# Hybrid gMLP/GLA encoder layer on one core: the first block's z weights split in three, three and two pieces, the low-rank part one slot later, the first output tile's product one slot sooner

## The chip, the cores and the metric

The kernel runs on one core of a Trainium2 chip. The metric is the device time of one execution in microseconds (us). The engines are PE (TensorE: matmuls), ACT (ScalarE), DVE (VectorE), POOL (GpSimd) and SP (SyncE, which here issues every transfer). Each works through its own instructions in order, so an instruction that waits also holds back everything behind it on its engine.

## The reference

One layer is applied to a prompt of 512 positions and to a sample of 2048, both 1024 wide:

```
h = rmsnorm(x) * norm_pre
p = h @ w_in                      # columns: u, v, z (512 each), q, k (256 each), v_b, z_b (512 each), lr_f, lr_b (16 each)
A = gelu(u) * (w_sp @ layernorm(gelu(v)) + b_sp) * silu(z)      # per chunk of 128 positions, 4 heads
g = log_sigmoid(lr @ w_gk + b_gk) / 16                          # forward and backward
B = rmsnorm(gla(q, k, v_b, g_f) + gla_reversed(q, k, v_b, g_b)) * silu(z_b)
y = x + rmsnorm(concat(A, B) @ w_out) * norm_post
```

## The kernel before

The 2560 positions are five blocks (b = 0 to 4) of 512. Every float32 operand of the large products is split into a high and a low float16 part, and three products (high by high, high by low, low by high) replace one. So a projection of 128 rows or 128 columns by 512 over the depth of 1024 is 24 matmuls of 128x512 (8 depth pieces by 3), which accumulate in one PSUM buffer.

`slot()` is the unit of the schedule, and it is written by hand. In each slot the generators already under way take one step each (older projections first, then pieces of weight preparation named by the table `pre`, then the list `early`, then `aux`, then the pieces named by `bg`), after that the slot's own projection is issued on PE, and last `flush()` issues the smaller matmuls that the steps have left in `late`. A step emits instructions in program order to every engine, so the slot at which a step runs fixes its place in each engine's queue.

The first block has 20 slots: z_b in slots 0 to 3, v_b 4 to 7, u 8 to 11, q/k 12 to 15 (`pqk`, column groups 0, 2, 1, 3), z 16 to 19 (`pz`). Later blocks have 24 slots: v (`pv`) 0 to 3, z_b (`pzb`) 4 to 7, v_b 8 to 11, q/k 12 to 15, then u and z in turn.

A projection writes to a buffer of the pool `pj`, which has two; the projection of slot s + 2 can start only when the buffer of slot s has been read out. The read-outs are: for q/k four `scalar_tensor_tensor` on DVE (L494, into the tiles QE and KE); for z a tanh on ACT (L447) and then a multiply on DVE (L448), after which POOL multiplies by gelu(u) (L449); one slot later DVE (L460, L462) joins this with the spatial product `sv`, and ACT squares it (L463) into the same buffer `th`, of which there is one.

In the first block the weights are also split. `g_wprep("z")` first finds a scale; then each of its eight steps splits one depth piece k of 128 rows: ACT writes the high part (L218), DVE the low part (L219). `pz` of slot 16 uses the pieces in the order k = 0 to 7, three matmuls each.

While block b runs, `g_xprep(b + 1, i)` prepares the next block's input for its four row tiles i. Its steps are: the load of x (L133); a square with a row sum on ACT (L119) that writes its unneeded result into the tile `xs`; a scaled copy on ACT (L138) into `xs`; the low part on DVE (L140), and two transposing transfers out of `xs` into `hT` (L129). The pool of x and xs has two buffers, so the square of tile i writes where the transposing transfers of tile i - 1 read. For block 1 the steps begin in slots 9, 12, 14 and 16 of block 0.

`g_lr` makes the low-rank part: 64 small matmuls (L511, `plr`), a copy on ACT (L517), some work with 16 transposes on DVE (L530), then copies into the tile `lr` (L534, L535), in three successive slots; `g_gates` multiplies `lr` by the gate weights (L558, `pg`) at the end of its first slot.

After block 4 the output projection follows: `g_out(t)` prepares output tile t (load, state, the product `oi` on PE, L797 and squares, then the products L809 to L815, which the table calls step five, then transposing transfers L819), and `g_main(t, n)` issues the 24 matmuls `py` (L844) for each half.

Of the kernel before, what the change touches and what calls it, by code (L numbers as in the profile page):

```python
# [35 lines left out]
def tile_hybrid_gmlp_gla(ctx: ExitStack, tc: tile.TileContext, x_prompt, x_sample, norm_pre, w_in,  # L36
# [359 lines left out]
    vb = [None] * NB  # L396
# [30 lines left out]
    def g_v(b, i):  # L427
        ps = proj_tok(b, i, W["v"], f"pv{b}_{i}")
        yield
        v = v_stats(b, i, v_gelu(b, i, ps, ("gu", "th")[i % 2]))  # L430
        yield
        v_split(b, i, *v)
# [36 lines left out]
    def g_zb(b, i):  # L469
        ps = proj_tok(b, i, W["zb"], f"pzb{b}_{i}")  # L470
        yield
        th = tp.tile([P, BT], F32, name=f"tb{b}_{i}", tag=TB_TAGS[b][i % len(TB_TAGS[b])])
        nc.scalar.activation(th, ps, AF.Tanh, scale=EVH["zb"])  # L473
        nc.vector.scalar_tensor_tensor(th, th, 1.0, ps, op0=ALU.add, op1=ALU.mult)  # L474
        yield
        nc.sync.dma_start(out=scr[b][:, i, 2, :], in_=th)

    def g_vb(b, i):
        ps = proj_tok(b, i, W["vb"], f"pvb{b}_{i}")
        yield  # L480
        if i == 0:
            vb[b] = bp.tile([P, 4, 512], F32, name=f"vb{b}", tag="big8")
        nc.scalar.activation(vb[b][:, i, :], ps, AF.Copy, scale=EV["vb"])

    def g_qk(b, c):
        ps = proj_ch(b, W["qk"], c * P, f"pqk{b}_{c}")
        yield
        dst = QE[b] if c < 2 else KE[b]
        s = EVH["qk"] if c < 2 else EV["qk"]
        for hh in range(2):  # L490
            h = 2 * (c % 2) + hh
            for d in range(2):
                o = dst[64 * d:64 * d + 64, h, :]
                nc.vector.scalar_tensor_tensor(o, ps[64 * hh:64 * hh + 64, :], s[64 * d:64 * d + 64], o,  # L494
                                               op0=ALU.mult, op1=ALU.mult)
        yield
        if c == 1:
            for i in range(4):
                nc.sync.dma_start(out=scr[b][:, i, 1, :].rearrange("p (h t) -> p h t", t=P),
                                  in_=QE[b][:, :, i * P:(i + 1) * P])  # L500
# [200 lines left out]
    def g_wout_bound(n, half, j):  # L701
        r = wout_piece(n, half, j, "wob")
        yield
        nc.scalar.activation(r, r, AF.Abs, scale=C["gnorm"] if half else 1.0,
                             accum_out=sumO[:, half, 2 * n + j:2 * n + j + 1])
# [117 lines left out]
    def out_step(t):  # L823
        if t < NT:
            if t not in outs:
                outs[t] = g_out(t)
            next(outs[t], None)
        return
        yield
# [222 lines left out]
    b = 0  # L1052
# [6 lines left out]
             16: [g_gla(b, 0), g_xprep(1, 3)], 18: [g_gla(b, 1)]}  # L1059
    first = {0: [g_v0_stats()], 5: [g_gates(b)]}  # L1060
    tiny = {0: ["vb"], 1: ["vb"], 2: ["u"], 3: ["u"], 5: ["qk", "sp"], 6: ["qk", "sp"], 10: ["z"], 12: ["z"]}
    pre = {2: [("vb", 4)], 3: [("vb", 5)], 13: [("z", 2)], 14: [("z", 2)], 15: [("z", 2)], 16: [("z", 2)]}
    plan = {1: [("u", 1)], 3: [("qk", 1)], 4: [("u", 4), ("qk", 1), ("sp", 1)], 5: [("u", 5)], 7: [("qk", 4)],
            8: [("qk", 5), ("sp", 1)], 9: [("sp", 2), ("z", 1)]}
    for s, u in enumerate(units):
# [7 lines left out]
    for b in range(1, NB):  # L1073
        units = ([g_v(b, i) for i in range(4)] + [g_zb(b, i) for i in range(4)] + [g_vb(b, i) for i in range(4)]
                 + [g_qk(b, c) for c in (0, 2, 1, 3)] + [f(b, h) for h in range(H) for f in (g_u, g_z)])
        extra = {}
        gates = {0: [g_lr(b)], 4: [g_gates(b)]}
        if b == 1:
            gates = {3: [g_lr(b)], 6: [g_gates(b)]}

        def at(s, *gens):
            extra.setdefault(s, []).extend(gens)

        chunks = [(b, i, 16 + 2 * i) for i in range(4)]
        if b == 1:
            chunks += [(0, 2, 0), (0, 3, 2)]
        for bb, i, s in chunks:
            at(s, g_gla(bb, i))
        if b in (1, 2):
            for s, piece in zip((19, 20, 21, 22), wo_pieces[4 * (b - 1):]):  # L1090
                at(s, g_wout_bound(*piece))
        if b == 3:
            at(12, g_wout_scale())
            for s, piece in zip((19, 20, 21, 22), wo_pieces):
                at(s, g_wout(*piece))
        if b < NB - 1:
            for i, s in enumerate((1, 6, 11, 15)):
                at(s, g_xprep(b + 1, i))
        else:
            for s, piece in zip((12, 13, 14, 15), wo_pieces[4:]):  # L1100
                at(s, g_wout(*piece))
            at(6, g_out_scale(0, NB - 1))
            at(14, g_npost())
            for s, t in ((17, 0), (18, 0), (19, 0), (19, 1), (20, 0), (20, 1), (21, 1), (22, 1), (22, 0), (23, 0)):
                at(s, out_step(t))
        for s, u in enumerate(units):
            if b == NB - 1 and s == 17:
                R3["OT"] = wp.tile([P, 4, KC, 2, P], F16, name="OT", tag="W")
            slot(u, new=extra.get(s, ()), first=gates.get(s, ()))
# [4 lines left out]
    for s in range(2 * NT):  # L1114
        t, n = s // 2, s % 2
# [43 lines left out]
```

## Time and profile before

| | |
|---|---|
| time, median of 3 runs | 980.91 us (980.67 to 981.34) |
| the profiled execution | 981.4 us, of which the span of the trace is 979.7 us |
| PE busy | 960.5 us, 98% of the span |
| DVE, ACT, POOL busy | 576.4, 418.9, 213.8 us |
| idle time of the matmul row, by what ended it | 5.9 us `pz` behind ACT's w_z; 1.0 and less for every other |

The busy time of PE is the sum of its matmul records, and a record runs on while the next begins. The rows of the sections below give a start, a length, the engine, the line, the operation and the tiles; in brackets stands the idle time of the engine before it and what ended that.

### The profile page before, as it was taken

Reading aid. Unit: us, or ns where it says so; the run is one execution under the profiler, and the core shown is the slowest. Engines: PE = TensorE matmul, PEld = TensorE weight load, DVE = VectorE, ACT = ScalarE, POOL = GpSimd, SP = SyncE. Lnnn points to the kernel's source line nnn. Section 1 sums busy time; section 2 is a strip of 40 time slices with the busy share of each in tenths; the row PEclk is TensorE's granted clock in tenths of the full one; section 3 lists DMA queues with packets and bytes.
Section 4 is the critical chain, followed back from the end, with each engine's and each line's share of the span. In section 5 each row is a group of like instructions: output and inputs, shape, how many; then the busy total and the mean of one; then the engine's idle time right before and its main releaser. Section 6 shows DMA issues by size and latency. Waiting matters only on the chain. (4 is left out here: it accounts for less than half of the span.)

```text
span 979.7 us, 14266 instructions
## 1 busy us (share of the span) xinstructions
PE 960.5 (98%) x5485; PEld 506.5 (52%) x5485; DVE 576.4 (59%) x1105; ACT 418.9 (43%) x795; POOL 213.8 (22%) x258
## 2 busy tenths in 40 slices
PE   8999979999999999999999999999999999999997
PEld 7744435654455544465544456444555545554444
DVE  6765764456655636655645757554666656566553
ACT  6779633534423363124363233353144344344341
POOL 1030202322011313021312112311123232322231
PEclk9999989999999999999999999999999999999999
DMA  9622134222332122333121332021415798767952
GB/s 321 227 71 80 44 86 108 96 89 55 86 108 91 61 76 65 86 108 108 43 86 43 87 118 87 33 76 44 172 65 199 216 260 258 223 220 224 248 163 97
DMA packets 113668, 120.71 MB, mean 123 GB/s; under 512 B 62784, under 2 KB 86208, under 8 KB 111040
## 3 DMA queue, kind: packets, MB, share of 16 engines
q1 hardware_dynamic: 113600, 119.80, 39.6%
q8 instruction: 43, 0.70, 0.3%
q14 instruction: 25, 0.20, 0.1%
HBM read 69.44 MB, written 36.70 MB: 108 GB/s over the span
## 5 line engine op out<-in xcount | busy, mean ns | idle before, releaser
L380 PEld LDWEIGHTS <-hT 128*128 128x128 f16 x1344 | 130.4, 98 | 157.5 <-issue 3.8
L844 PE MATMUL py<-wo,OT 128*128 128x512 f16 (+1 forms) x960 | 207.9, 376 | 0.0
L844 PEld LDWEIGHTS <-OT 128*128 128x128 f16 x984 | 96.3, 98 | 106.9
L390 PE MATMUL pz<-hT,w_z 128*128 128x512 f16 x480 | 108.5, 382 | 5.9 <-ACT w_z L218 5.9
L380 PE MATMUL pzb<-w_zb,hT 128*128 128x512 f16 x480 | 106.4, 379 | 1.0 <-DVE tb L474 1.0
L390 PE MATMUL pu<-hT,w_u 128*128 128x512 f16 x480 | 106.6, 379 | 0.0
L390 PE MATMUL pqk<-hT,w_qk 128*128 128x512 f16 x480 | 105.1, 379 | 0.5 <-DVE KE L494 0.5
L380 PE MATMUL pvb<-w_vb,hT 128*128 128x512 f16 x480 | 104.8, 379 | 0.0
L637 DVE STREAM_TRANSPOSE kt<-KE 32x128 f32<-32x128 f32 x224 | 67.8, 303 | 34.4 <-PE kv L671 31.4
L380 PE MATMUL pv<-w_v,hT 128*128 128x512 f16 x384 | 84.5, 379 | 0.4 <-ACT vf L406 0.4
L449 POOL TENSOR_TENSOR th<-th,gu 128x512 f32<-128x512 f32 x20 | 32.7, 1635 | 211.3 <-DVE th L448 211.3
L390 PEld LDWEIGHTS <-w_z 128*128 128x128 f16 x480 | 45.8, 98 | 60.8 <-ACT w_z L218 6.4
L390 PEld LDWEIGHTS <-w_qk 128*128 128x128 f16 x480 | 46.7, 98 | 56.7 <-DVE KE L494 1.0
L390 PEld LDWEIGHTS <-w_u 128*128 128x128 f16 x480 | 47.0, 98 | 55.9
L863 DVE TENSOR_TENSOR y<-py,npost 128x512 f32<-128x512 f32 (+1 forms) x40 | 27.4, 685 | 70.6 <-PE py L844 60.2
L463 ACT ACTIVATE th<-t 128x512 f32<-128x512 f32 x20 | 12.6, 630 | 129.9 <-DVE t L462 129.7
L860 ACT ACTIVATE junk<-py 128x512 f16<-128x512 f32 (+1 forms) x40 | 23.7, 591 | 85.7 <-DVE y L863 84.5
L474 DVE SCALAR_TENSOR_TENSOR tb<-tb,pzb 128x512 f32<-128x512 f32 x20 | 13.7, 687 | 56.5 <-ACT tb L473 56.4
L494 DVE SCALAR_TENSOR_TENSOR QE<-pqk,ev_qk,QE 64x512 f32<-64x512 f32 x40 | 30.0, 749 | 27.3 <-PE pqk L390 24.3
L590 POOL TENSOR_TENSOR KE<-QE 64x1024 f32<-64x1024 f32 x10 | 32.1, 3210 | 63.4 <-DVE QE L584 40.4
L119 ACT ACTIVATE xs<-x 128x1024 f16<-128x1024 f32 x16 | 16.8, 1051 | 62.7 <-DMA x<-in_x_sample_dram 28.4
L654 DVE COPY_PREDICATED pr<-jlec,X 128x512 f32<-128x512 int32 x20 | 14.6, 730 | 40.7 <-ACT pr L653 40.5
(310 smaller groups left out, 1359.6 us busy)
## 6 DMA issues: line engine op xcount, KB each, us to landing
L<-scr SPq DMA_DIRECT2D x20, 1280.0 KB, 6.7
out_dram<-y SPq DMA_DIRECT2D x19, 512.0 KB, 7.4
x<-in_x_sample_dram SPq DMA_DIRECT2D x16, 512.0 KB, 4.1
xres<-in_x_sample_dram SPq DMA_DIRECT2D x16, 512.0 KB, 8.2
scr<-tb SPq DMA_DIRECT2D x20, 256.0 KB, 2.0
scr<-QE SPq DMA_DIRECT2D x20, 256.0 KB, 3.1
scr<-t SPq DMA_DIRECT2D x20, 256.0 KB, 2.4
scr<-S SPq DMA_DIRECT2D x20, 256.0 KB, 2.0
```

The lines of the kernel that those rows point to most:

```text
L119: nc.scalar.activation(junk, xt, AF.Square, accum_out=ms)
L380: nc.tensor.matmul(ps, lhsT=hT[b][:, k, a, i * P:(i + 1) * P], rhs=w[:, k, c, :], start=(n == 0), stop=(n == 3 * KC - 1))
L390: nc.tensor.matmul(ps, lhsT=w[:, k, c, col:col + P], rhs=hT[b][:, k, a, :], start=(n == 0), stop=(n == 3 * KC - 1))
L449: nc.gpsimd.tensor_tensor(t, t, gus[b, h], op=ALU.mult)
L474: nc.vector.scalar_tensor_tensor(th, th, 1.0, ps, op0=ALU.add, op1=ALU.mult)
L494: nc.vector.scalar_tensor_tensor(o, ps[64 * hh:64 * hh + 64, :], s[64 * d:64 * d + 64], o, op0=ALU.mult, op1=ALU.mult)
L590: nc.gpsimd.tensor_tensor(Mv[64:128, h:h + 2], Av[64:128, h:h + 2, :, ::-1], mid[64:128, h:h + 2].to_broadcast([64, 2, 4, P]), op=ALU.subt ...
L637: nc.vector.transpose(out=kt[32 * c:32 * c + 32, :, d], in_=KE[b][d, :, i * P + 32 * c:i * P + 32 * c + 32])
L654: nc.vector.copy_predicated(pr, C["jmask"], X)
L844: nc.tensor.matmul(bank[:, cs], lhsT=OT[:, k, a, :], rhs=wo[n][:, k, c, cs], start=(m == 0), stop=(m == 3 * KC - 1))
L860: nc.scalar.activation(junk[:, cs], pss[j][:, cs], AF.Square, accum_out=ms[:, n + j:n + j + 1])
L863: nc.vector.tensor_tensor(y[:, n * 512:(n + 1) * 512][:, cs], pss[j][:, cs], npost[n][:, cs], op=ALU.mult)
```

## The change

Three edits of the slot tables.

```diff
-    pre = {2: [("vb", 4)], 3: [("vb", 5)], 13: [("z", 2)], 14: [("z", 2)], 15: [("z", 2)], 16: [("z", 2)]}
+    pre = {2: [("vb", 4)], 3: [("vb", 5)], 13: [("z", 3)], 14: [("z", 3)], 15: [("z", 2)]}
...
-        gates = {0: [g_lr(b)], 4: [g_gates(b)]}
+        gates = {1: [g_lr(b)], 4: [g_gates(b)]}
         if b == 1:
             gates = {3: [g_lr(b)], 6: [g_gates(b)]}
...
-            for s, t in ((17, 0), (18, 0), (19, 0), (19, 1), (20, 0), (20, 1), (21, 1), (22, 1), (22, 0), (23, 0)):
+            for s, t in ((17, 0), (18, 0), (19, 0), (19, 1), (20, 0), (20, 1), (21, 0), (21, 1), (22, 0), (22, 1)):
                 at(s, out_step(t))
```

The first edit moves z's pieces. On ACT, slots 13 to 17 of block 0, before (xs_1, xs_2 are row tiles 1 and 2 of block 1, w_z the pieces' high parts, th_0 the tanh of the first `pz`):

```order
L218 ACTIVATE w_z<-raw_z,nps_z 128x512 x2
L119 ACTIVATE xs_1_1313,xms_1_1314<-x_1_1266 128x1024
L218 ACTIVATE w_z<-raw_z,nps_z 128x512 x2
L138 ACTIVATE xs_1_1313<-x_1_1266,xms_1_1314 128x1024
L218 ACTIVATE w_z<-raw_z,nps_z 128x512 x2
L119 ACTIVATE xs_2_1390,xms_2_1391<-x_2_1352 128x1024
L218 ACTIVATE w_z<-raw_z,nps_z 128x512 x2
L138 ACTIVATE xs_2_1390<-x_2_1352,xms_2_1391 128x1024
L447 ACTIVATE th_0_1476<-pz_0_1439,ev_z 128x512
```

And with the change:

```order
L218 ACTIVATE w_z<-raw_z,nps_z 128x512 x3
L119 ACTIVATE xs_1_1315,xms_1_1316<-x_1_1266 128x1024
L218 ACTIVATE w_z<-raw_z,nps_z 128x512 x3
L138 ACTIVATE xs_1_1315<-x_1_1266,xms_1_1316 128x1024
L218 ACTIVATE w_z<-raw_z,nps_z 128x512 x2
L119 ACTIVATE xs_2_1394,xms_2_1395<-x_2_1356 128x1024
L138 ACTIVATE xs_2_1394<-x_2_1356,xms_2_1395 128x1024
L447 ACTIVATE th_0_1476<-pz_0_1439,ev_z 128x512
```

The last two pieces have moved from behind the square of row tile 2 to ahead of it. On DVE in the same slots, before (KE, QE: the read-outs of `pqk`; w_z the low parts):

```order
L219 SCALAR_TENSOR_TENSOR w_z<-raw_z,nps_z,w_z 128x512 x2
L608 TENSOR_TENSOR wst<-ab 64x12
L611 TENSOR_TENSOR wst<-ab 64x12
L494 SCALAR_TENSOR_TENSOR KE_974<-pqk_2_1318,ev_qk,KE_974 64x512 x4
L219 SCALAR_TENSOR_TENSOR w_z<-raw_z,nps_z,w_z 128x512 x2
L494 SCALAR_TENSOR_TENSOR QE_973<-pqk_1_1354,ev_qk,QE_973 64x512 x4
L219 SCALAR_TENSOR_TENSOR w_z<-raw_z,nps_z,w_z 128x512 x2
L140 SCALAR_TENSOR_TENSOR xs_1_1313<-x_1_1266,xms_1_1314,xs_1_1313 128x1024
L494 SCALAR_TENSOR_TENSOR KE_974<-pqk_3_1395,ev_qk,KE_974 64x512 x4
L219 SCALAR_TENSOR_TENSOR w_z<-raw_z,nps_z,w_z 128x512 x2
L448 SCALAR_TENSOR_TENSOR th_0_1476<-th_0_1476,pz_0_1439 128x512
```

And with the change:

```order
L219 SCALAR_TENSOR_TENSOR w_z<-raw_z,nps_z,w_z 128x512 x3
L608 TENSOR_TENSOR wst<-ab 64x12
L611 TENSOR_TENSOR wst<-ab 64x12
L494 SCALAR_TENSOR_TENSOR KE_974<-pqk_2_1320,ev_qk,KE_974 64x512 x4
L219 SCALAR_TENSOR_TENSOR w_z<-raw_z,nps_z,w_z 128x512 x3
L494 SCALAR_TENSOR_TENSOR QE_973<-pqk_1_1358,ev_qk,QE_973 64x512 x4
L219 SCALAR_TENSOR_TENSOR w_z<-raw_z,nps_z,w_z 128x512 x2
L140 SCALAR_TENSOR_TENSOR xs_1_1315<-x_1_1266,xms_1_1316,xs_1_1315 128x1024
L494 SCALAR_TENSOR_TENSOR KE_974<-pqk_3_1399,ev_qk,KE_974 64x512 x4
L448 SCALAR_TENSOR_TENSOR th_0_1476<-th_0_1476,pz_0_1439 128x512
```

One low part more stands ahead of the first KE, two ahead of QE, and two ahead of the low part of xs_1 and the second KE. The second edit, on ACT in slots 1 to 3 of block 4, before (vf: the read-outs of `pv`, two halves each; lrt and lr: the low-rank part; va: the float16 copies of vf):

```order
L406 ACTIVATE vf_0_5391<-pv_0_5278,ev_v_445 128x256
L517 ACTIVATE lrt_5401<-plr_5271,ev_lr 128x256
L682 ACTIVATE S_5274<-kv_5276 64x512
L684 ACTIVATE ob_5430<-o_5277 128x512
L424 ACTIVATE va_5458<-vf_0_5391 128x512
L406 ACTIVATE vf_1_5462<-pv_1_5432,ev_v_252 128x256
L406 ACTIVATE vf_1_5462<-pv_1_5432,ev_v_445 128x256
L534 ACTIVATE lr_5410<-lrtr_5411 64x512
L424 ACTIVATE va_5458<-vf_1_5462 128x512
```

And with the change:

```order
L406 ACTIVATE vf_0_5326<-pv_0_5277,ev_v_445 128x256
L682 ACTIVATE S_5273<-kv_5275 64x512
L684 ACTIVATE ob_5339<-o_5276 128x512
L424 ACTIVATE va_5431<-vf_0_5326 128x512
L406 ACTIVATE vf_1_5435<-pv_1_5341,ev_v_252 128x256
L406 ACTIVATE vf_1_5435<-pv_1_5341,ev_v_445 128x256
L517 ACTIVATE lrt_5445<-plr_5336,ev_lr 128x256
L424 ACTIVATE va_5431<-vf_1_5435 128x512
```

The copy out of `plr` now stands behind the second read-out of v instead of the first; its matmuls and DVE's 16 transposes move likewise, in blocks 2, 3 and 4 alone.

## Rows read from the trace of the kernel before

**Rows 1.** The page: the span, and the busy time of the engines with their share of it and their instructions.

```profile
span 979.7 us, 14266 instructions
PE 960.5 (98%) x5485; PEld 506.5 (52%) x5485; DVE 576.4 (59%) x1105; ACT 418.9 (43%) x795; POOL 213.8 (22%) x258
```

**Rows 2.** The waits of PE: who waited for whom, us in total, how often, longest.

```profile
PE pz L390 <- ACT w_z L218: 5.9, 1, 5.9
...
PE pqk L390 <- DVE KE L494: 0.5, 1, 0.5
PE pv L380 <- ACT vf L406: 0.4, 1, 0.4
```

**Rows 3.** The timeline of PE's matmuls, block 0 slots 15 to 19 and the first slots of block 1: start, length, instruction, count.

```profile
127.29 5.35 PE L390 MATMUL pqk<-hT,w_qk 128*128 128x512 f16 x24 [0.47 <-DVE KE L494]
132.48 4.05 PE L390 MATMUL pz<-hT,w_z 128*128 128x512 f16 x18
142.46 2.74 PE L390 MATMUL pz<-hT,w_z 128*128 128x512 f16 x6 [5.94 <-ACT w_z L218]
...
147.66 5.34 PE L390 MATMUL pz<-hT,w_z 128*128 128x512 f16 x24
...
153.51 5.34 PE L390 MATMUL pz<-hT,w_z 128*128 128x512 f16 x24
...
161.29 0.37 PE L642 MATMUL X<-QE,KE 64*128 64x128 f32 x1
...
162.88 5.34 PE L390 MATMUL pz<-hT,w_z 128*128 128x512 f16 x24
...
168.73 5.34 PE L380 MATMUL pv<-w_v,hT 128*128 128x512 f16 x24
...
178.09 10.52 PE L380 MATMUL pv<-w_v,hT 128*128 128x512 f16 x48
```

**Rows 4.** Stretches of one us: PE, PEld, DVE, ACT, POOL busy with counts, then the clock granted to PE (1.00 is 2.4 GHz), the transfers' share and their GB/s.

```profile
48.00:49.00 1.00, 0.43 (x4) 0.43 (x5) 0.97 (x3) 0.00 (x0) 0.52 (x3) 1.00 0.00 0
139.00:140.00 1.00, 0.00 (x0) 0.00 (x0) 0.00 (x0) 0.00 (x0) 0.00 (x0) 1.00 1.29 267
140.00:141.00 1.00, 0.00 (x0) 0.00 (x0) 0.00 (x0) 0.35 (x1) 0.00 (x0) 0.70 1.15 346
147.00:148.00 1.00, 1.00 (x9) 0.70 (x7) 0.95 (x2) 0.74 (x2) 1.00 (x1) 0.88 0.00 0
```

**Rows 5.** The timeline of ACT from block 0 slot 13 to block 1 slot 0, with one instruction of POOL (the root of the row sum, between the square and the scaled copy).

```profile
121.75 1.33 ACT L218 ACTIVATE w_z<-raw_z,nps_z 128x512 f16<-128x512 f32 x2 [1.70 <-DVE nps_z L209]
...
140.65 1.06 ACT L119 ACTIVATE xs<-x 128x1024 f16<-128x1024 f32 x1 [13.03 <-DMA hT<-xs]
...
142.16 0.55 POOL L124 TENSOR_TENSOR xms<-xms,neghalf 128x1 f32<-128x1 f32 x1
...
142.93 1.13 ACT L138 ACTIVATE xs<-x,xms 128x1024 f16<-128x1024 f32 x1
145.24 0.69 ACT L447 ACTIVATE th<-pz,ev_z 128x512 f32<-128x512 f32 x1 [1.18 <-PE pz L390]
...
154.06 1.06 ACT L119 ACTIVATE xs<-x 128x1024 f16<-128x1024 f32 x1 [5.60 <-DMA hT<-xs]
155.02 0.19 ACT L119 ACTIVATION_READ_ACCUMULATOR xs<-x 128x1 f32 x1
155.35 0.63 ACT L463 ACTIVATE th<-t 128x512 f32<-128x512 f32 x1
...
156.10 0.69 ACT L447 ACTIVATE th<-pz,ev_z 128x512 f32<-128x512 f32 x1
...
171.50 0.69 ACT L447 ACTIVATE th<-pz,ev_z 128x512 f32<-128x512 f32 x1
```

**Rows 6.** The timeline of DVE in the same stretch.

```profile
122.51 1.42 DVE L219 SCALAR_TENSOR_TENSOR w_z<-raw_z,nps_z,w_z 128x512 f16<-128x512 f32 x2 [0.73 <-ACT w_z L218]
...
127.26 1.42 DVE L219 SCALAR_TENSOR_TENSOR w_z<-raw_z,nps_z,w_z 128x512 f16<-128x512 f32 x2
128.69 3.04 DVE L494 SCALAR_TENSOR_TENSOR QE<-pqk,ev_qk,QE 64x512 f32<-64x512 f32 x4
131.76 1.41 DVE L219 SCALAR_TENSOR_TENSOR w_z<-raw_z,nps_z,w_z 128x512 f16<-128x512 f32 x2
133.10 1.28 DVE L140 SCALAR_TENSOR_TENSOR xs<-x,xms,xs 128x1024 f16<-128x1024 f32 x1
...
146.57 1.28 DVE L140 SCALAR_TENSOR_TENSOR xs<-x,xms,xs 128x1024 f16<-128x1024 f32 x1
...
156.82 0.69 DVE L448 SCALAR_TENSOR_TENSOR th<-th,pz 128x512 f32<-128x512 f32 x1 [1.51 <-ACT th L447]
```

**Rows 7.** The timelines of DVE, ACT and PE, block 4 slots 1 to 4.

```profile
613.92 5.05 DVE L530 STREAM_TRANSPOSE lrtr<-lrk 32x128 f32<-32x128 f32 x16 [0.27 <-POOL lrk L523]
...
621.40 0.83 ACT L406 ACTIVATE vf<-pv,ev_v 128x256 f32<-128x256 f32 x2
...
632.45 0.81 PE L558 MATMUL pg<-lr,wg 128*128 128x512 f32 x2
```

**Rows 8.** The timeline of SP, the first output tile's transposing transfers; and the chain that ended last, the first matmuls of the output projection.

```profile
737.53 2.75 SPq L819 DMA_TRANSPOSE OT<-L  x2
...
747.68 5.18 PE py L844 x24
```

## Prediction

> **What bounds the kernel now.** I read the busy times first: PE is busy for 960.5 of 979.7 us [rows 1], so a change pays only where it removes time in which PE stands or runs slowly. The waits of PE came next: apart from the opening they hold one of any size, 5.9 us of `pz` behind ACT's w_z; those behind DVE's KE (0.5) and ACT's vf (0.4) are small [rows 2]. PE's timeline shows the place: the first `pz` starts at 132.48, stops after 18 of its 24 matmuls, which is six of eight depth pieces, and goes on at 142.46 after 5.94 us idle [rows 3]. ACT's timeline shows what is late: ACT stood for 13.03 us before the square of row tile 2 of block 1, which started at 140.65 and was released by the transposing transfers out of xs_1; the last two w_z pieces stand right behind it in program order. So the pieces were not dear, they were queued behind an instruction that waits for a transfer.
>
> The stop costs more than its length. The granted clock fell from 1.00 (2.4 GHz) towards 0.50 (1.2 GHz) at about 140.4 and was back late in 147 to 148 [rows 4]. From the start of the first `pz` to that of the second is 147.66 - 132.48 = 15.18 us [rows 3]. At full clock it is 5.19 (127.29 to 132.48, one projection start to start) plus the X, Y and transpose matmuls, 161.29 to 162.88 = 1.59 [rows 3], so 6.78. The loss is 8.40 us: 5.94 standing, 2.46 slow.
>
> **First edit: z in 3, 3, 2.** The number of instructions is the same; their places move. On ACT a piece takes 1.33 / 2 = 0.67 [rows 5]. ACT begins them at 121.75 and has no wait ahead of it until the square of tile 2, so all eight high parts, one square and one scaled copy end near 129. The 5.94 and the slow stretch go: + 8.40.
>
> The price is on DVE, which is the engine behind PE in these slots: its rows run on with hardly a gap from 122.51 [rows 6]. Three terms follow.
>
> (a) One low part more (1.42 / 2 = 0.71, with overlap 0.67) stands ahead of the first KE read-out. The `pqk` that starts at 127.29 was already waiting for that read-out (0.47) [rows 2, 3], so it starts 0.67 later, at 127.96, and the first `pz` at 133.15. QE follows two low parts later, 128.69 + 1.3 = 130.0 to 133.1; its buffer is the one that `pz` needs, so it comes just in time. Cost 0.67.
>
> (b) Two low parts more stand ahead of xs_1's low part, which starts 1.3 later than its 133.10 [rows 6]. From that instruction to ACT's next square is 140.65 - 133.10 = 7.55, and again 154.06 - 146.57 = 7.49 for the next tile, a chain of SP transfers [rows 5, 6]. So the square of tile 2 moves to 141.95. POOL's root ends 142.71 - 140.65 = 2.06 after its start [rows 5], hence the scaled copy at 144.0 and, 1.1 later, the tanh of the first `pz` at 145.1. From tanh to DVE's product is 0.72 and that takes 0.69 [rows 5, 6]: the buffer is free at 146.5. PE is at the third `pz` at 133.15 + 6.78 + 5.85 (147.66 to 153.51 [rows 3]) = 145.8. It waits 0.8 and starts at 146.6.
>
> (c) xs_2's low part follows the product at about 146.45, nearly its old 146.57, so the square of tile 3 still starts near 153.9. Behind it stand the squared z (1.15 later, no longer waiting for DVE), the second tanh 0.75 later and the product: the buffer is free at 157.25. PE is there at 146.6 + 9.37 (153.51 to 162.88) = 156.0. It waits 1.3; the fourth `pz` starts at 157.3 instead of 162.88, and `pv` 5.85 later at 163.15 instead of 168.73.
>
> Balance: 8.40 - 0.67 - 0.8 - 1.3 = 5.6. Bounds of (b) and (c): nothing, if the two squares find their tiles free early, which the 7.5 us of both rows speak against; and one us more for each if the transfers, now nearer to PE's own pace, run slower: 5.6 becomes 8 or 3.6.
>
> What is late next is the z read-outs of block 0 against `pv`. The fourth tanh ran at 171.50 [rows 5] and freed its buffer at 172.9, 5.2 ahead of the `pv` at 178.09 [rows 3]. PE comes 5.6 sooner, so with no move of that chain there would be 0.4 of waiting; the chain starts sooner by the third tile's share, so I take nothing and keep 1 us as the bound.
>
> **Second edit: low-rank part in slot 1, blocks 2 to 4.** The same 64 matmuls, copies and 16 transposes run one slot later. In block 4 DVE's transposes (5.05 from 613.92) held up DVE's part of v's first tile, ACT's va behind it and so the second vf, 621.40 [rows 7], for which the fourth `pv` waited 0.4 [rows 2]. In slot 2 the same 5 us hold up the third vf instead. I place the transposes some 4.6 later, at 618.5 (a projection of 5.19 later, less what stood ahead of them in slot 1). Before, the vf started 621.40 - 613.92 = 7.48 behind them and ran 0.83 [rows 7]; with the same spacing the third vf ends at 626.8, and the projection that needs its buffer comes at about 627.0. The spacing should shrink, since a state update and two copies that stood between stay in slot 1. So + 0.36, and nothing in blocks 2 and 3, where PE did not wait. What hides the delay of `lr` itself is the time to `pg` at 632.45 [rows 7]: `lr` is copied right behind that vf, some 627, with about 5 us left. Bounds: 0.4 gained in block 4, to 0.3 lost in each of the three.
>
> **Third edit.** Five DVE, two ACT and one POOL instruction and two transfers move one slot up. Before, the transfers were issued at 737.53 and `py` began at 747.68 without a wait [rows 8]: nothing to gain. They move ahead of the third z read-out on ACT and DVE and may delay it by 1 to 2 us, but its buffer is next used two slots (over 10 us) later. 0.
>
> **Sum.** 5.6 + 0.36 = 6.0. The profiled execution, 981.4 with its span of 979.7 [rows 1], would become 975.4; it stood 0.5 above the median, 980.91, so the median goes to 974.9.
>
> **A rule against this.** Two rows show waits of PE for a read-out of one of two `pj` buffers, 0.5 and 0.4 [rows 2]; terms (b) and (c) are such waits too. The Trainium skill, Perfetto Trace Analysis, section Optimization Strategy, says that a gap repeating on the engine that should be saturated can mean too little PSUM for the next tile. By it alone the wait would change its place and not go, and the sum could fall to the third rival's. In the trace before no such gap repeats through this stretch.
>
> **Rivals.**
> 1. The buffers are free in time (terms b and c vanish): gain 8.40 - 0.67 + 0.36 = 8.1, median 972.8. For it: ACT is idle for most of the stretch. Against: the same squares still wait for the same transfers.
> 2. The clock falls again in the new waits. One fall cost 2.46, so 977.4. Against: the 0.57 us that PE stood within 48 to 49 left the clock at 1.00, and the fall here came some 3.9 us after PE stopped [rows 4].
> 3. The wait only changes its place: `pz` gets its weights, but the blocked squares hold the read-outs, so that PE loses 6.8 us or more in (a) to (c) instead of 2.8: 979 to 981, no measurable change. It needs the xs chain 4 us later than in (b); DVE gives only 1.3.
> 4. Slower: `lr` is late in blocks 2, 3 and 4 and PE stands at `pg` in each. From no measurable change up to + 2 us, each block must lose (6.0 + 2) / 3 = 2.7, on top of the 5 us in hand: the chain of copy, transposes and copy must come 7.7 us later than I place it, more than a slot; then 983. Nothing in block 1, which runs the same chain over the same three slots, shows that.
>
> **Numbers.** Forecast, with new waits of 1 to 4.5 us: chance 0.75. Rival 1: 0.09. Rival 2: 0.07. Rival 3: 0.07. Rival 4: 0.02. A difference of 0.2% (2 us) is about what a measurement of this kernel can tell from none. Faster: 0.91 (forecast, rivals 1 and 2); same 0.07; slower 0.02. Predicted 974.9; the range 972.9 to 977.8 holds the forecast with its bounds, rival 2 and the edge of rival 1.
>
> **What would show it.** Right: no wait of `pz` for w_z; a granted clock of 1.00 through 136 to 150; waits of PE for KE or QE of about 1.1, for the third and fourth `pz` behind DVE's product of about 0.8 and 1.3; `pv` of block 1 near 163.2; no wait for vf in block 4, and none for `lr` at any `pg`. Wrong: a fourth `pz` that starts after 159, a half clock in block 0, or a repeated wait at the start of blocks 2 to 4.

## The result, and the profile after

The changed kernel took 975.6 us in the median of four runs (975.55, 975.59, 975.61 and 977.29), the kernel before 981.12 beside it (980.67 to 981.34): the ratio is 0.9948, with a 95% interval of 0.9931 to 0.9966. Forecast were 974.9, within 972.9 to 977.8. In the experiments two slow executions, 1006.82 us of the first edit alone (the profiled one) and 2598.57 us with both tiles late, are left out of the medians; with it counted in, the latter median would be 978.88, the figure that a later expectation names, and not 978.67.

The profiled execution is the long one, 977.29. Its page, span and busy times:

```profile
span 975.6 us, 14272 instructions
...
PE 958.7 (98%) x5485; PEld 504.7 (52%) x5485; DVE 575.2 (59%) x1105; ACT 419.0 (43%) x795; POOL 214.0 (22%) x258
```

Against [rows 1] PE is busy for 1.8 us less (its busy time is the time that at least one matmul record covers, not the sum of the records), DVE for 1.2 less, ACT and POOL for the same within 0.2. The span of this execution is 975.6; those of the other three are 973.8, 973.9 and 973.8, so its 1.8 us need a place. Its PE timeline (start, length, instruction, count, and in brackets the idle time before and what ended it) has them at the fourth `pz`:

```profile
157.72 7.03 PE L390 MATMUL pz<-hT,w_z 128*128 128x512 f16 x24 [2.03 <-DVE th L448]
...
165.25 5.34 PE L380 MATMUL pv<-w_v,hT 128*128 128x512 f16 x24
```

The fourth `pz` waited 2.03 us for DVE's product, then took 7.03 us where a `pz` takes 5.34 [rows 3]. Stretches of one us of the same execution (PE, PEld, DVE, ACT, POOL busy with counts, then PE's granted clock, transfer share, GB/s):

```profile
158.00:159.00 1.00, 1.00 (x5) 0.43 (x4) 0.33 (x1) 0.00 (x0) 1.00 (x2) 0.67 0.00 0
159.00:160.00 1.00, 1.00 (x3) 0.30 (x2) 0.75 (x1) 0.17 (x1) 0.47 (x2) 0.50 0.96 219
161.00:162.00 1.00, 1.00 (x5) 0.33 (x4) 0.69 (x2) 0.27 (x1) 0.00 (x0) 0.62 0.00 0
```

The granted clock fell from 1.00 (2.4 GHz) to 0.50 (1.2 GHz) soon after 158 and came back before 162; 7.03 - 5.34 = 1.7 us were lost by that. The last experiment has a second profile of this kernel; that execution (975.29, span 973.6; the median of the five executions there is 977.45) has no such fall, and the rows of after that answer to [rows 2, 3, 5, 6] are taken from it. Waits of PE:

```profile
PE pz L390 <- DVE th L448: 1.6, 2, 1.1
```

The 5.9 us of `pz` for w_z and the 0.4 of `pv` for vf of [rows 2] are gone; what is new is 1.6 in two waits for DVE's product, 0.7 more for KE (1.14 against 0.47), and 0.2 of a `pzb` in block 1. PE's timeline:

```profile
127.86 5.35 PE L390 MATMUL pqk<-hT,w_qk 128*128 128x512 f16 x24 [1.14 <-DVE KE L494]
133.11 5.34 PE L390 MATMUL pz<-hT,w_z 128*128 128x512 f16 x24
...
139.97 5.34 PE L390 MATMUL pz<-hT,w_z 128*128 128x512 f16 x24
...
146.46 5.34 PE L390 MATMUL pz<-hT,w_z 128*128 128x512 f16 x24 [0.48 <-DVE th L448]
...
157.08 5.34 PE L390 MATMUL pz<-hT,w_z 128*128 128x512 f16 x24 [1.09 <-DVE th L448]
...
162.92 5.34 PE L380 MATMUL pv<-w_v,hT 128*128 128x512 f16 x24
```

The first `pz` now runs through all 24 matmuls. The second starts 6.86 behind it, not 15.18 as in [rows 3]; `pv` of block 1 starts at 162.92, 5.81 sooner than before. From there to the end are 973.6 - 162.92 = 810.7 us, and before 979.7 - 168.73 = 811.0. So nearly all of the gain lies ahead of block 1; what lies behind it is a loss and a gain, taken apart below at the second edit.

### The profile page after: what moved, and what is told of

Read it like the earlier page. It is cut to its first block, busy times and chain, and to the rows that moved or that the text cites. A ratio compares the mean times of both kernels' runs of the same rounds, so it can differ in the third digit from the quotient of the medians.

```text
span 975.6 us, 14272 instructions
## 1 busy us (share of the span) xinstructions
PE 958.7 (98%) x5485; PEld 504.7 (52%) x5485; DVE 575.2 (59%) x1105; ACT 419.0 (43%) x795; POOL 214.0 (22%) x258
## 4 chain that ended last, share of the span: by engine, by line
PE 86%; ACT 4%; issue 3%; DVE 3%; DMA 1%; POOL 1%; SPq 0%; POOLq 0%; DVEq 0%; ACTq 0%
PE py L844 20%; PE pvb L380 10%; PE pz L390 9%; PE pzb L380 9%; PE pqk L390 9%; PE pv L380 8%; PE pu L390 8%; PE X L642 2%; PE oi L792 2%; PE kv L671 2%; PE o L674 2%; PE sv L455 1%; DMA hT<-xs 1%; PE plr L511 1%; PE pv L954 1%
```

## The experiments

All ratios are against the kernel before on the same chip, whose median stood between 980.99 and 981.21 beside these runs.

### The three edits, each alone

First edit alone (z in 3, 3 and 2 pieces):

```
-    pre = {..., 13: [("z", 2)], 14: [("z", 2)], 15: [("z", 2)], 16: [("z", 2)]}
+    pre = {..., 13: [("z", 3)], 14: [("z", 3)], 15: [("z", 2)]}
```

> The first edit alone (z in 3, 3, 2), the other two undone. Theory one, that nearly all of the gain is the two w_z pieces leaving their place behind the blocked square: 5.2 us less than before (about 975.9), with the wait of 0.4 us for vf in block 4 still there. Rival, that the low-rank part or the output tile carry a visible share: a gain of 4 us or less here.

Measured: 976.0 (975.96 to 976.16), ratio 0.9952 (0.9938 to 0.9965). The first edit brings 5.0 us, where all three brought 5.5. That the wait for vf in block 4 is still there, as the expectation says, no trace of this kernel shows.

Second edit alone (low-rank part of blocks 2 to 4 in slot 1 instead of 0):

```
-        gates = {0: [g_lr(b)], 4: [g_gates(b)]}
+        gates = {1: [g_lr(b)], 4: [g_gates(b)]}
```

> The second edit alone (low-rank part in slot 1 of blocks 2 to 4). Theory one: 0.4 us less than before, by the wait for vf in block 4 that goes; no wait at pg. Rival: the transposes of DVE hold up the third read-out of v instead, and the time is the same or up to 0.5 us more.

Measured: 980.79 beside 980.99, ratio 0.9999 (0.9990 to 1.0008). The time can't tell it from nothing. Its trace can: the wait of `pv` for vf in block 4 is gone, and PE waits for nothing new in blocks 2 to 4. The first `pv` of block 2, in the timeline of PE before:

```profile
317.51 5.34 PE L380 MATMUL pv<-w_v,hT 128*128 128x512 f16 x24
```

And in this kernel:

```profile
318.29 5.34 PE L380 MATMUL pv<-w_v,hT 128*128 128x512 f16 x24
```

From there to the end are 979.7 - 317.51 = 662.2 us before and 979.8 - 318.29 = 661.5 with the edit. The other traces read here agree: 662.1 in the two other kernels without it (the third edit alone, and the kernel before with later tiles), 661.5 in each of the nine others with it. So the edit saves 0.6 us behind block 1. The changed kernel's short execution has its `pv` of block 2 at 312.06: it too takes 661.5 from there, but for block 1 it takes 312.06 - 162.92 = 149.1, and before that was 317.51 - 168.73 = 148.8.

Third edit alone (first output tile a slot sooner):

```
-  ..., (20, 0), (20, 1), (21, 1), (22, 1), (22, 0), (23, 0)
+  ..., (20, 0), (20, 1), (21, 0), (21, 1), (22, 0), (22, 1)
```

> The kernel before with the third edit alone (the first output tile's product and its transfers one slot sooner). Theory one (its transfers were hidden: py began without a wait): nothing, 980.9 +- 0.4, and no new wait of PE at py. Rival: the moved instructions hold up the third z read-out of the last block, and PE waits for it: 1 to 2 us slower, 982 to 983.

Measured: 981.22 beside 981.21, ratio 1.0001 (0.9992 to 1.0009): nothing, as expected. Its trace agrees: from the first `pv` of block 4 to the end it takes 979.8 - 602.11 = 377.7 us, the trace of before 979.7 - 601.93 = 377.8.

### Do the three terms add? z in 2, 2 and 4 pieces

```
-    pre = {..., 13: [("z", 3)], 14: [("z", 3)], 15: [("z", 2)]}
+    pre = {..., 13: [("z", 2)], 14: [("z", 2)], 15: [("z", 4)]}
```

> The changed kernel with z in 2, 2 and 4 pieces over slots 13 to 15, so that DVE's first KE and QE read-outs are not delayed. Theory one, that the fourth pz is timed by the chain of row tiles (low part of xs_1, transfers, square, tanh) and not by the sum of the waits: the wait for KE falls from 1.2 to 0.5, pz starts 0.7 sooner, the waits of the third and fourth pz grow by 0.7 together, and the time is that of the changed kernel within 0.3 us. Rival, that each low part ahead of a read-out costs its own time: 0.7 us less than the changed kernel.

Measured: 975.61, ratio 0.9949 (0.9935 to 0.9962), the same as the changed kernel. PE's timeline of this kernel:

```profile
146.57 5.34 PE L390 MATMUL pz<-hT,w_z 128*128 128x512 f16 x24 [0.92 <-DVE th L448]
...
157.42 5.34 PE L390 MATMUL pz<-hT,w_z 128*128 128x512 f16 x24 [1.32 <-DVE th L448]
...
163.27 5.34 PE L380 MATMUL pv<-w_v,hT 128*128 128x512 f16 x24
```

With two pieces in slot 13 the KE read-out is early again (PE waits 0.48 for it, as in [rows 2]), but `pv` starts no sooner: what (a) saved comes back as 0.92 and 1.32 of waiting for the two products. So (a), (b) and (c) of the prediction are not three costs side by side. The chain of the row tiles (low part, transfers, square, read-out) sets when the third and the fourth `pz` may start, and PE meets that chain early or late.

### The square of tile 3 taken out of the read-out's way

The changed kernel, with row tile 3 of block 1 begun in slot 17 instead of 16:

```
-             16: [g_gla(b, 0), g_xprep(1, 3)], 18: [g_gla(b, 1)]}
+             16: [g_gla(b, 0)], 17: [g_xprep(1, 3)], 18: [g_gla(b, 1)]}
```

> The changed kernel with the preparation of row tile 3 of block 1 begun in slot 17 instead of 16, so that its square stands behind the second tanh of z on ACT. Theory one, that this square holds up the read-out which the fourth pz waits for: that wait (2.0 us in the profiled execution) is gone, and with it any fall of the clock there; 1.3 to 2.0 us less than the changed kernel, about 973.9. Rival, that DVE's load sets the read-out: no change.

Measured: 974.95 (974.78 to 975.61), ratio 0.9942 (0.9930 to 0.9955): 0.65 less than the changed kernel, not the 1.3 or more of the first theory. The two intervals overlap, so the times alone do not tell the kernels apart; the trace does. PE's timeline of this kernel:

```profile
155.81 5.34 PE L390 MATMUL pz<-hT,w_z 128*128 128x512 f16 x24
...
161.66 5.34 PE L380 MATMUL pv<-w_v,hT 128*128 128x512 f16 x24
...
205.07 5.34 PE L380 MATMUL pzb<-w_zb,hT 128*128 128x512 f16 x24 [0.92 <-DVE tb L474]
```

The fourth `pz` no longer waits, and `pv` is at 161.66, 1.3 sooner than 162.92. But in block 1 a `pzb` now waits 0.92 for a zb read-out. ACT's timeline of this kernel at that place:

```profile
203.09 0.63 ACT L424 ACTIVATE va<-vf 128x512 f16<-128x512 f32 x1 [8.74 <-DVE vf L422]
203.62 0.67 ACT L473 ACTIVATE tb<-pzb,ev_zb 128x512 f32<-128x512 f32 x1
```

The read-out (203.62) stands on ACT behind `va`, which had waited 8.74 us for DVE. DVE's timeline of this kernel there:

```profile
196.17 5.05 DVE L530 STREAM_TRANSPOSE lrtr<-lrk 32x128 f32<-32x128 f32 x16 [0.27 <-POOL lrk L523]
```

The 16 transposes of block 1's low-rank part take 5.05 us of that wait. PE came 1.3 us earlier to a chain that came less early: this `pzb` starts at 205.07, and in the short execution of the changed kernel at 205.53. Most of the gain went there.

### Is it the place of the square? The kernel before with only tiles 2 and 3 later

```
-             ..., 14: [g_xprep(1, 2)], 16: [g_gla(b, 0), g_xprep(1, 3)], ...
+             ..., 15: [g_xprep(1, 2)], 16: [g_gla(b, 0)], 17: [g_xprep(1, 3)], ...
```

> The kernel before with z still in 2, 2, 2 and 2 pieces over slots 13 to 16, and only row tiles 2 and 3 of block 1 begun one slot later (slots 15 and 17 instead of 14 and 16), so that on ACT all eight w_z pieces stand ahead of the square that waits for the transfers. Theory one (the 5.94 us and the slow clock came from the place of that square, not from how the pieces are divided): the wait of pz for w_z is gone or under 1.5 us, the clock stays at 1.00, and the time is 974 to 976, that is all of the first edit's gain without its split. Rival (the division of the pieces over the slots is what matters; with 2 in slot 16 they come too late whatever stands ahead of them): pz still waits 4 us or more, 979 to 981.

Measured: 980.15 (979.69 to 980.44), ratio 0.9989 (0.9981 to 0.9998). PE's timeline of this kernel:

```profile
137.92 1.05 PE L390 MATMUL pz<-hT,w_z 128*128 128x512 f16 x4 [1.33 <-DVE w_z L219]
...
162.62 5.34 PE L380 MATMUL pv<-w_v,hT 128*128 128x512 f16 x24 [0.90 <-DVE th L448]
...
180.37 6.84 PE L380 MATMUL pv<-w_v,hT 128*128 128x512 f16 x24 [3.04 <-ACT vf L406]
```

Two stretches of this kernel, with the columns of the stretches above:

```profile
180.00:182.00 2.00, 1.63 (x4) 0.56 (x4) 1.58 (x4) 0.32 (x1) 0.47 (x1) 0.51 0.00 0
182.00:184.00 2.00, 2.00 (x7) 0.80 (x6) 0.23 (x2) 1.88 (x4) 0.08 (x1) 0.64 0.22 85
```

On the wait the first theory was right: with z still in four times two pieces, the stop inside the first `pz` is 1.33 us instead of 5.94 (and what it waits for is now DVE's low part, not ACT's high part), the clock stays at 1.00 through it, and `pv` of block 1 is at 162.62, as soon as in the changed kernel. On the time it was wrong by 4 to 6 us: the third `pv` stands 3.04 us for its buffer, and then runs 6.84 instead of 5.34, at a clock of 0.51 and 0.64. The place of the square made the old wait; moving the tiles makes another one, 40 us later.

### Both tiles late in the changed kernel

```
-             ..., 14: [g_xprep(1, 2)], 16: [g_gla(b, 0), g_xprep(1, 3)], ...
+             ..., 15: [g_xprep(1, 2)], 16: [g_gla(b, 0)], 17: [g_xprep(1, 3)], ...
```

> The changed kernel with row tiles 2 and 3 of block 1 both begun one slot later. Theory one (both waits of pz behind DVE's product come from squares that stand ahead of the z read-outs): no wait of pz behind th is left, pv of block 1 starts near 161.2 (161.66 with tile 3 alone late), but the wait for the first zb read-out in block 1, 0.92 with tile 3 alone late, takes back the 0.4: 974.5 to 975.0. Rival (that wait of zb is no bound of its own): 974.95 less 0.4, 974.5 or less, with the zb wait no longer than 0.9.

Measured: 978.67 (978.32 to 980.09), ratio 0.9977 (0.9969 to 0.9986): 3.7 us slower than with tile 3 alone late. Both theories had missed it. The wait of the third `pv` that the run before this one showed stands in its trace too, and the way to it can be read back. PE's timeline of this kernel:

```profile
180.27 7.03 PE L380 MATMUL pv<-w_v,hT 128*128 128x512 f16 x24 [3.02 <-ACT vf L406]
```

It is the first v read-out that is late. ACT's timeline of this kernel:

```profile
178.08 1.28 ACT L406 ACT_TABLE_LOAD   x1
179.38 0.84 ACT L406 ACTIVATE vf<-pv,ev_v 128x256 f32<-128x256 f32 x2
```

The read-out started at 179.38 behind a table load, and that stood behind the square of `t` of the last head (177.36). DVE's timeline of this kernel, where that `t` is written:

```profile
175.72 0.75 DVE L460 SCALAR_TENSOR_TENSOR t<-sv,gv,bsp 128x512 f32<-128x512 f32 x1 [4.24 <-DMA scr<-t]
```

DVE had waited 4.24 us to write it, since there is one buffer for `t` (the tag `t3`), until the `t` before it was stored. The transfers on SP's queue (SPq) of this kernel:

```profile
165.38 7.36 SPq L129 DMA_TRANSPOSE hT<-xs  x2
172.78 0.60 SPq L465 DMA_DIRECT2D scr<-t  x1
```

That store was issued at 172.78, behind 7.36 us of transposing transfers of tile 3. But this wait alone does not tell the two kernels apart. With tile 3 alone late DVE waits as long at that place, and the read-out comes 4 us sooner all the same. DVE's timeline of that kernel, then ACT's:

```profile
171.72 0.75 DVE L460 SCALAR_TENSOR_TENSOR t<-sv,gv,bsp 128x512 f32<-128x512 f32 x1 [4.29 <-DMA scr<-t]
```

```profile
175.39 0.84 ACT L406 ACTIVATE vf<-pv,ev_v 128x256 f32<-128x256 f32 x2
```

What differs is a wait of the same kind two heads earlier. DVE's timeline with both tiles late:

```profile
158.66 0.75 DVE L460 SCALAR_TENSOR_TENSOR t<-sv,gv,bsp 128x512 f32<-128x512 f32 x1 [7.09 <-DMA scr<-t]
```

That `t` waited 7.09 us for a store which SP's queue took up at 155.88, behind the transposing transfers of tile 2 (3.81 us from 152.03), and the chain was 4 us late from there on: tile 3's transfers begin at 165.38, and with tile 3 alone late at 161.34.

### Low-rank part of block 1 a slot sooner

On top of the run before, to take the transposes out of the way of zb's read-out:

```
-            gates = {3: [g_lr(b)], 6: [g_gates(b)]}
+            gates = {2: [g_lr(b)], 6: [g_gates(b)]}
```

> As the run with both tiles late, and besides block 1's low-rank part begins in slot 2 instead of 3, so that its 16 transposes on DVE (5.05 us) no longer stand between the last v read-out and the first zb read-out. Theory one (those transposes cause the 0.9 us wait of the second-next zb projection): that wait is gone and the time is 0.9 to 1.3 less than with both tiles late, 973.4 to 974.0. Rival (the transposes hold up the third v read-out instead, and PE waits for its buffer): a wait of pv or pzb behind vf of 0.5 us or more in its place, no difference.

Measured: 979.84, ratio 0.9988 (0.9979 to 0.9996), 1.2 more, not 0.9 less. The expectation rested on a wait that wasn't there: with both tiles late PE had lost 4.7 us at the third `pv`, and the zb read-out of block 1 was no longer late. Of the 1.2, 0.43 is a new wait of a `pzb` at 210.0; the rest is not settled (the two profiled executions are only 0.4 apart).

### Three buffers for t

The run with both tiles late, and the `t` of the second and the fourth head in the tiles where `gu` of their own head lay, free by then (the expectation calls it the tanh input; it is the gelu output that the tanh is multiplied by). No instruction moves:

```
-        t3 = tp.tile([P, 4, P], F32, ..., tag="t3")
+        t3 = tp.tile([P, 4, P], F32, ..., tag=("t3", "gm", "t3", "gs")[h] if b == 0 else "t3")
```

> As the run with both tiles late (978.88), and besides the four t tiles of block 0 get three buffers instead of one (the second and the fourth lie where the tanh input of their own head lay, which is free by then). No instruction moves on any engine. Theory one (in the runs with both tiles late, t waited for the store of the t before it, which stands on the SP queue behind 7.4 us of transposing transfers, and with it the tanh table load and the first v read-out of block 1, so that PE stood 3.0 us before the third pv and ran it slowly): that wait is gone, the clock stays at 1.00, and the first pv no longer waits 1.2 us for the third z read-out: 5 to 6 us less, 973 to 974.5. Rival (the chain of transfers itself comes too late, whatever t waits for): the third pv still waits 2 us or more, 977 to 979.

Measured: 974.26 (974.15 to 974.68), ratio 0.9931 (0.9918 to 0.9943): 4.4 less for nothing but two buffers. PE's timeline of this kernel:

```profile
170.43 10.56 PE L380 MATMUL pv<-w_v,hT 128*128 128x512 f16 x48
...
204.46 5.34 PE L380 MATMUL pzb<-w_zb,hT 128*128 128x512 f16 x24 [0.94 <-DVE tb L474]
```

The second and third `pv` run in one piece. No `t` of block 0 waits for a store any more: the two that had waited 7.09 and 4.24 us are written at 152.50 and 171.10. ACT's first v read-out in this kernel:

```profile
174.76 0.84 ACT L406 ACTIVATE vf<-pv,ev_v 128x256 f32<-128x256 f32 x2
```

It starts at 174.76 instead of 179.38. What is left is the `pzb` wait of block 1, 0.94, which the run with both tiles late had hidden. This shows the cause: a buffer whose release is a store that stands behind transposing transfers.

### Tile 3 late and the low-rank part sooner, without and with the buffers

Without:

> As the run with tile 3 alone late (974.95), and besides block 1's low-rank part begins in slot 2 instead of 3. Theory one (the 16 transposes of 5.05 us are what held up the first zb read-out there): the 0.92 us wait of pzb falls to 0.4 or less, 974.0 to 974.6. Rival (the transposes then hold up the third v read-out and PE waits for its buffer instead): a wait of pv or pzb for vf of 0.5 us or more, 974.8 to 975.5.

Measured: 976.65, ratio 0.9953 (0.9940 to 0.9965), 1.7 more than with tile 3 alone late. PE's timeline of this kernel:

```profile
176.79 5.34 PE L380 MATMUL pv<-w_v,hT 128*128 128x512 f16 x24 [0.37 <-ACT vf L406]
...
198.62 1.16 PE L671 MATMUL kv<-vb,kt 128*128 128x128 f32 x8 [0.84 <-ACT kt L656]
```

The wait of this `pv` for vf, 0.37, comes 5 us before the first instruction of the low-rank part (its matmuls begin at 181.97), so the edit did not make it. It goes back to the transposing transfers of tile 2, which held SP's queue for 4.55 us here and for 3.72 with tile 3 alone late: the load of tile 3 behind them and the square that waits for it, the `t` after that and the v read-out came 0.5 us later. Nothing ahead of that place moves with the edit, so this part of the 1.7 is not shown to be its price. A `kv` waits for a copy by ACT, which waits for DVE. DVE's timeline of this kernel:

```profile
189.55 5.05 DVE L530 STREAM_TRANSPOSE lrtr<-lrk 32x128 f32<-32x128 f32 x16 [0.27 <-POOL lrk L523]
194.63 0.68 DVE L681 TENSOR_TENSOR U<-kv,S 64x512 f32<-64x512 f32 x1
```

The 5.05 us of transposes now stand ahead of DVE's state update (194.63). ACT's timeline of this kernel behind it:

```profile
195.35 0.59 ACT L682 ACTIVATE S<-kv 64x512 f32<-64x512 f32 x1 [7.62 <-DVE U L681]
```

ACT waits 7.62 for the update, its copy of the transposed keys comes late behind that, and PE waits 0.84 for it, and 0.77 at the third `pzb`. The wait has changed its place once more. Both theories missed: the 0.92 of `pzb` fell to 0.77 only, and the rival's wait, of a buffer behind the transposes, isn't there; the edit's loss stands in a row that neither named.

With three buffers for `t`:

> The changed kernel with tile 3 alone late, block 1's low-rank part in slot 2 and three buffers for t in block 0. Theory one (with tile 3 alone late the store of t is not behind the transposes for long enough to matter to PE: the third pv started without a wait): the same as without the t buffers to 0.5 us. Rival (the first v read-out of block 1 is what sets PE's start of the third pv there, though it shows no wait): 0.5 to 1.5 us less, near 973.2. Either way it should be the fastest of these kernels, 973.0 to 974.6.

Measured: 973.76 (four of five within 973.5 to 973.8, one 975.53), ratio 0.9928 (0.9915 to 0.9942). This is the lowest median found, though its interval overlaps that of the run with both tiles late and three buffers. Its PE timeline has no wait in block 1:

```profile
171.01 10.52 PE L380 MATMUL pv<-w_v,hT 128*128 128x512 f16 x48
...
198.80 10.52 PE L380 MATMUL pzb<-w_zb,hT 128*128 128x512 f16 x48
```

The first theory (no difference from the run without) is wrong by 2.9 us. The rival, by which the first v read-out of block 1 sets PE's pace, has the direction, at more than its 0.5 to 1.5: that read-out starts at 171.66 here and at 175.90 without the buffers, and the waits of 0.37, 0.84 and 0.77 that stood there are all gone. Against tile 3 alone late, 974.95, the two edits together save 1.2, and the low-rank edit without the buffers loses 1.7.

### The changed kernel once more

> The changed kernel once more, since its profiled execution (977.3) was 1.7 us longer than its other three (975.6) and shows a fall of the clock at 158 to 162 behind a wait of 2.03 us. Theory one (that fall belongs to that execution, in which the second of two transfer chains took 8.45 us instead of about 7.5): a profile with a span near 973.8, waits of the third and fourth pz of 0.4 to 0.9 and about 1.3 us, the clock at 1.00 from 120 to 190, and pv of block 1 near 163.3; times near 975.6. Rival (the fourth pz always waits 2 us and the clock falls in every execution, and the other three gained elsewhere): the same fall at 158 to 162 and pv near 165.2 in a profile whose span is 973.8.

Measured: 975.25, 975.29, 977.45, 977.46 and 977.64, so that the median is 977.45 here, ratio 0.9958 (0.9944 to 0.9972). With the first four runs, nine executions fall in two groups, five at 975.25 to 975.61 and four at 977.29 to 977.64, none between; the median of the nine is 975.61. The profiled one is of the short group (rows above): span 973.6, waits of 0.48 and 1.09, clock 1.00 from 120 to 190. The theory is right on what such an execution looks like; that the long one is rare was wrong, it is four of nine. Only one long execution has a profile. The two differ in the transposing transfers of xs_2. SP's queue in the long execution:

```profile
147.75 4.50 SPq L129 DMA_TRANSPOSE hT<-xs  x2
```

And in the short one:

```profile
148.05 3.55 SPq L129 DMA_TRANSPOSE hT<-xs  x2
```

They held the queue for 4.50 us and for 3.55. From xs_2's low part to the square of tile 3 it is 8.45 (146.02 to 154.47) against 7.50 (146.32 to 153.82), and PE's wait behind it is 2.03 against 1.09. That the other three long executions have the same cause is likely, since they are as long and their granted clocks, as means over the span, are 0.998, 0.997 and 0.997 (the profiled long one 0.998, the short ones 0.998 to 1.0), but it is not shown. Nor is it shown why those transfers take longer. They were longer in other kernels too, 4.55 and 4.59 us in the two profiles with tile 3 late and the low-rank part sooner, against 3.55 to 3.94 in the other ones read here; with tile 3 late its square no longer stands ahead of the z read-out, and no fall of the clock followed.

## Why the prediction was right

**The stop and the slow clock (+ 8.40).** Both went: the second `pz` starts 6.86 behind the first; 6.78 was worked out. The run with the old split and later tiles shows the cause as told: the pieces were queued behind a square that waits for a transfer. Taking it away, without touching the split, left 1.33 of 5.94, and that for DVE.

**(a), KE late (0.67).** PE waits 1.14, against 0.47 + 0.67.

**(b) and (c), the row tiles.** The short execution follows the forecast closely. DVE's timeline of it:

```profile
145.72 0.69 DVE L448 SCALAR_TENSOR_TENSOR th<-th,pz 128x512 f32<-128x512 f32 x1 [6.98 <-ACT th L447]
146.32 1.28 DVE L140 SCALAR_TENSOR_TENSOR xs<-x,xms,xs 128x1024 f16<-128x1024 f32 x1
```

And ACT's, the squares of tiles 2 and 3 and the tanh of the first `pz`:

```profile
141.87 1.06 ACT L119 ACTIVATE xs<-x 128x1024 f16<-128x1024 f32 x1 [13.13 <-DMA hT<-xs]
...
145.02 0.67 ACT L447 ACTIVATE th<-pz,ev_z 128x512 f32<-128x512 f32 x1
...
153.82 1.06 ACT L119 ACTIVATE xs<-x 128x1024 f16<-128x1024 f32 x1 [7.17 <-DMA hT<-xs]
```

The square of tile 2 was placed at 141.95 and came at 141.87, the tanh at 145.1 and came at 145.02, the square of tile 3 near 153.9 and came at 153.82. The fourth `pz` was placed at 157.3 and `pv` at 163.15; they started at 157.08 and 162.92. The waits are shown as 0.48 for 0.8 and 1.09 for 1.3. A row counts idle time from the end of the record before it, and the prediction from the time at which the `pz` would have started: without a wait a projection's record of 5.34 overlaps the next, which starts 5.19 later [rows 3], and a wait loses that overlap, some 0.16, as well. Counted as the prediction does, from 139.97 + 5.85 and from 146.46 + 9.37, the two cost 0.64 and 1.25.

**What was put wrongly.** The balance subtracts (a), (b) and (c) from the stop as if each could be saved by itself. The run with z in 2, 2 and 4 shows that they can't: saving (a) lengthened the others by as much. The 5.6 is right because its times were followed along the chain, not because its terms are separate. That 0.36 on top of it gave the right 6.0 for the profiled executions (979.7 - 973.6 = 6.1) is in part luck: the second edit brought 0.6 and block 1 lost 0.4.

**What is late next.** The 0.4 of z read-outs against `pv` was taken as nothing, and in the changed kernel PE waits for nothing there. What came late next is the zb read-out in block 1, which the prediction did not name: a `pzb` waits 0.2 for it, and block 1 takes 0.4 longer than before. The experiments show how close that is: 1.3 us sooner a `pzb` waits 0.92, and with the tiles a slot later the third `pv` stands 3.0 us.

**Second edit (0.36).** Right in its place, too small in its size: the vf wait of block 4 is gone, and from block 2 to the end the kernel takes 0.6 us less. The 0.36 is the idle time alone. With the overlap that a wait loses it is 0.53: before, the three `pv` of which the last waits took 627.46 - 611.39 = 16.07 us, and with the edit alone two take 627.61 - 617.25 = 10.36, so three 15.54. The rest, under 0.1, is not accounted for. DVE's timeline of the short execution, to be held against [rows 7] as the two after it (ACT and DVE each copy a half of `lr`):

```profile
612.79 5.05 DVE L530 STREAM_TRANSPOSE lrtr<-lrk 32x128 f32<-32x128 f32 x16 [0.18 <-POOL lrk L523]
...
621.01 0.42 DVE L535 CAST lr<-lrtr 64x512 fp32r<-64x512 f32 x1
```

ACT's, with the third vf:

```profile
619.03 0.82 ACT L406 ACTIVATE vf<-pv,ev_v 128x256 f32<-128x256 f32 x2
```

PE's, the first `pg`:

```profile
626.37 0.82 PE L558 MATMUL pg<-lr,wg 128*128 128x512 f32 x2
```

Block 4 begins 5.52 ahead of before (596.41 against 601.93), so in the times of before the transposes start at 618.3 (618.5 was worked out), and the third vf ends at 625.4, not 626.8: the spacing shrank. The later copy into `lr` ends 4.9 us ahead of `pg`, where about 5 was worked out. In the times of the run with this edit alone 0.6 us is below what can be told; it is shown by the traces.

**Third edit (0).** Nothing, by its own run.

**Rival 2, the clock.** It had 7 in 100, and it happens in some executions: by the one profile, a fall behind a wait of 2.03 us that costs 1.7, and 977.4 was its time, where the long group lies at 977.3 to 977.6. That the time agrees so well is in part luck: the fall cost 1.7 and not 2.46, and the rest is the longer wait, which the prediction had among its bounds for (c), as one us more if the transfers run slower. The step that failed for these executions is the argument against a fall, that the one of before came 3.9 us after PE had stopped, beside 0.57 us of standing that did no harm. The fall in the long execution came 2.7 us after PE had stopped, when PE was at work again. No standstill between 0.57 and 5.94 us stood in the rows that the prediction went by.

**The median.** 974.9 against 975.6. The profiled execution of before stood 0.5 above the median of its runs, and that was taken off the forecast too; the changed kernel's short executions, 975.25 to 975.61, lie around the 975.4 that was worked out for a profiled one. So the offset was the term that failed there, by 0.5. Of the later five executions the median, 977.45, is of the long group; it lies within the range because the range took in rival 2, not because the forecast held for it.

**The rule of the Trainium skill** (Perfetto Trace Analysis, section Optimization Strategy) is that a gap repeating on the engine that should be saturated can mean too little SBUF or PSUM for the next tile. The prediction told it of PSUM alone, which would have made the waits a matter of buffers of `pj`. What runs here show is that the wait of the fourth `pz` went when the square moved, with the same PSUM. With both tiles late the buffers which were short lay in SBUF, the `t` with its store, and two more of them took away the 3.02 us of the third `pv`; that is the kind of cause that the Trainium skill names, though the gap stood there once and did not repeat.

## What to carry to other kernels

Work queued on an in-order engine behind an instruction that waits for a transfer is late by that transfer, however cheap it is; look at what the waiting instruction is before splitting the work behind it. In a kernel that is 98% bound by one engine, follow times along the chain that meets it, and don't add costs that lie on the same chain. Each gain runs until the next late read-out; here a start 1.3 us sooner met a new wait of 0.92. Count a wait at more than its idle time, here by 0.16 us, for the overlap of two matmuls that is lost with it. A buffer released by a store is released when the queue comes to that store, so see what stands ahead of it.

## What the hardware showed unexpectedly

- The clock fell to 0.50 for some 3.4 us behind 2.03 us without work on PE, at about 158.3, when PE had already started again and 2.7 us after it had stopped; in [rows 4] it fell 3.9 us after PE had stopped. Waits of 1.09 to 1.33 us left it at 1.00.
- The same two transposing transfers of one row tile held the queue for 3.55 and 4.50 us in two executions of one program. The kernel has two groups of times, 1.9 us apart, and the one profile of the longer group shows that delay and the slow matmuls behind it.
